# A hybrid decoder layer on one core: fixed buffers for the gated values, the merge's product in halves, and another place for a norm's iteration

## The chip, the cores and the metric

The kernel runs on one core of a Trainium2 chip. Its time is the device time of one execution in microseconds. An execution drives five engines, each with its own queue of instructions that it works through in order: TensorE (PE in the profile; its weight loads are PEld), VectorE (DVE), ScalarE (ACT), GpSimd (POOL) and SyncE (SP). SyncE and GpSimd issue the DMA transfers.

## The reference

One decoder layer for 1024 prompt tokens and 8 single decode tokens, 1032 in all, in float32, with model width 1024 and FFN width 2816:

```python
def swiglu_half(x, g, w_gate, w_up, w_down):
    u = rmsnorm(x, g)
    return x + 0.5 * ((jax.nn.silu(u @ w_gate) * (u @ w_up)) @ w_down)
...
    h = swiglu_half(x, lp['ffn1_norm'], lp['ffn1_w_gate'], lp['ffn1_w_up'], lp['ffn1_w_down'])
    u = rmsnorm(h, lp['mix_norm'])
    z = u @ lp['w_in']
...
    merged = (jax.nn.sigmoid(ga) * (o_att @ lp['w_branch_att'])
              + jax.nn.sigmoid(gr) * (o_ret @ lp['w_branch_ret']))
    h = h + merged @ lp['w_out']
    h = swiglu_half(h, lp['ffn2_norm'], lp['ffn2_w_gate'], lp['ffn2_w_up'], lp['ffn2_w_down'])
    gate = jax.nn.sigmoid(rmsnorm(h, lp['ple_norm']) @ lp['w_ple_gate'])
    h = h + gate * (p_emb @ lp['w_ple_proj'])
```

Between the first FFN and the merge stand latent attention and retention, which the change doesn't touch; a final norm ends the layer.

## The kernel before

Activations lie transposed, features on the 128 partitions and tokens along the free dimension. The tokens are in two halves of 516, `tp` 0 and 1, and each half in two pieces of `HC` = 258 columns, so that a piece fills one of the 8 PSUM banks. A float32 product is made of three matmuls (high by high, high by low, low by high); ScalarE takes the high part of a weight row (L106) and VectorE the low part (L107). `Rows` and `Stream` hold the weights that are ahead: SyncE fetches a raw row (L317, into one of 8 buffers of a pool), it is split into one of 6 `w` buffers, and `take` hands it out.

**The FFN block** (class `Block`, run twice, as block 1 and block 2). Its first two of 22 feature blocks go through a plain product, in four steps n = 0 to 3 that are (l, tp) = (0,0), (1,0), (1,1), (0,1) (L562 to L564); the others go through `unit`, a product by a Strassen-like scheme with 7 instead of 8 multiplications (L337 to L340), whose operands are sums of token blocks, made on VectorE (L509 to L517) and split (L107) into `b0` for tp 0 and `b1` for tp 1. The RMS norm's scale is applied to the results. `norm(tp)` has two steps: the first sums the squares on TensorE (L355) and finds the inverse root by an iteration of twelve tiny steps on VectorE (L357, L146 to L150); the second spreads it over the partitions by TensorE (L364) and copies it to `r` by ScalarE (L366). The norm of tp 1 takes its first step ahead of step n = 2 and its second behind n = 2's products.

The gated values are written to HBM, `mid_d`, from four `s` tiles (L541), since they don't fit beside the operands. The down product (`product`, L384 to L386) reads them back as 22 tiles `m` of 516 KB each: for tp 0 GpSimd fetches them, f = 0 first, and for tp 1 SyncE, each into the buffer that tp 0 has done with (L703). For each f the product makes 24 matmuls, three for each of 8 banks. The pool of the `m` tiles is opened when `b0`, `b1`, the x1 copy of the tokens and the `s` tiles are closed, and lies over them; a fetch waits until what lay at its buffer's place has been used for the last time.

**The merge** makes the gated mix of the two branches (L1453, L1454), keeps it for tp 0 in SBUF and writes it for tp 1 to HBM (`mg_d`). Its product with `w_out` runs for each tp over four quarters of 256 output columns, four banks each, in 8 steps f. After the first quarter of tp 0 it asks for all eight operands of tp 1 (`operand`, L1420) and for tp 1's residual (`residual`, L1424). A quarter's results are added to the residual (L1484) and stored to `h2_d` (L1486). While tp 1 is multiplied, the norm, the tokens' scaling (L499) and the sums of tp 0 for block 2 are made step by step.

The order on each engine comes from a scheduler of the framework, which works from the order of the program and its own estimates; at run time each engine keeps that order.

Of the kernel before, what the change touches and what calls it, by code (L numbers as in the profile page):

```python
# [10 lines left out]
F32 = mybir.dt.float32  # L11
F32R = mybir.dt.float32r
# [8 lines left out]
P = 128  # L21
D = 1024
KT = D // P
# [6 lines left out]
NF = DFF // P  # L30
# [19 lines left out]
HC = T // 4  # L50
TPS = (0, 1)
# [5 lines left out]
def body(ctx, tc, a):  # L57
# [370 lines left out]
    class Block:  # L428
# [100 lines left out]
        def run(self, nxt, nxt_st, prepare, accs=None, load=None, more=None):  # L529
# [38 lines left out]
                return self.pe.tile([P, HC], F32, tag="p", name="p")  # L568

            for n, (l, tp) in enumerate(((0, 0), (1, 0), (1, 1), (0, 1))):  # L570
                norm = None
                if n == 2 and accs[tp] is not None:
                    norm = self.norm(tp, accs[tp])
                    next(norm)
                if n == 0 and not begun:
                    rows.ahead, ws, pg = 0, [], []
                    for lr in range(2):
                        load(0, lr)
                        self.fresh(0, lr)
                        ws += [rows.take() for _ in range(2)]  # L580
                        pg.append(plain(ws[:2], 0, lr))
                    load(1, None)
                    squared(0)
                    rows.ahead = 3
                else:
                    if n != 2:
                        ws = [rows.take() for _ in range(4)]
                    pg = [plain(ws[:2], tp, lr) for lr in range(2)]
                if n == 0 and accs[tp] is not None:
                    norm = self.norm(tp, accs[tp])  # L590
                    next(norm)
                pu = [plain(ws[2:], tp, lr) for lr in range(2)]
                if norm:
                    next(norm)
                ts = []
                for lr in range(2):
                    t = pt()
                    ts.append(t)
                    dve.tensor_tensor(t, pg[lr][:, :HC], self.r[tp][:, HV[lr]], op=ALU.mult)
                    act.activation(t, t, AF.Silu)  # L600
                for lr in range(2):
                    dve.tensor_tensor(ts[lr], pu[lr][:, :HC], ts[lr], op=ALU.mult)
                    put(0, tp, l, lr, ts[lr])
                if n == 0:
                    if not begun:
                        squared(1)
                    for _ in self.plain_tokens(1):
                        pass
                elif n == 1:
                    if not begun:  # L610
                        self.scaled(0)
                        for _ in self.sums(0):
                            pass
                    self.last_sum(0)
                elif n == 2:
                    for _ in self.sums(1):
                        pass
# [77 lines left out]

            nxt.open()
            m_st = ExitStack()
            mp = m_st.enter_context(pools(pre + "m", NF, side="right"))
            mids = {}

            def fetch(tp, f):
                mids[tp, f] = t = mp.tile([P, 2, 2 * HC], F32R, tag="m", name="m")
                self.loaded = (sp if tp else pool).dma_start(t.bitcast(F32), self.mid_d[f, tp])  # L703

            for f in range(NF):
                fetch(0, f)
            with pools(pre + "h", 2) as hp, pools(pre + "t", 2) as tmp:
                for tp in TPS:
                    for o in range(2):
                        ht = hp.tile([P, 4, 2 * HC], F32, tag="h", name="h")  # L710

                        def each(f):
                            if f == 4:
                                sp.dma_start(ht, self.src[:, 4 * o:4 * o + 4, both(tp)])
                            if (tp, o) == (0, 1):
                                fetch(1, f)

                        end = tp == 1 and o == 1
                        if end:
                            next(nxt.norms[0])  # L720
                        banks = product(rows, lambda f: mids[tp, f], NF, 4, each)
                        if tp == 1 and o == 0:
                            with tc.issue_after(self.loaded.ins):
                                nxt.first = prepare(nxt.ring)
                        if end:
                            m_st.close()
                            nxt.open_u(nxt_st)
                            nxt.fetch()
                            next(nxt.norms[0])
                        for n in range(8):  # L730
                            hv = ht[:, n // 2, HV[n % 2]]
                            t = tmp.tile([P, HC], F32, tag="c", name="c")
                            dve.scalar_tensor_tensor(t, banks[n][:, :HC], 0.5, self.r[tp][:, HV[n % 2]],
                                                     op0=ALU.mult, op1=ALU.mult)
                            dve.tensor_tensor(hv, hv, t, op=ALU.add)
                            if n % 2:
                                k = 4 * o + n // 2
                                sp.dma_start(self.dst[:, k:k + 1, both(tp)], ht[:, n // 2:n // 2 + 1])
                        if tp == 1 and o == 0:
                            held = ht  # L740
                        if end:
                            for k in range(4):
                                nxt.row(tmp, 1, k, held[:, k])
                        for k in range(4):
                            if tp == 0 or end:
                                nxt.row(tmp, tp, 4 * o + k, ht[:, k])
                        for k in range(4):
                            nxt.squares(tmp, tp, 4 * o + k, ht[:, k], dve if end else pool)
                        if end and more:
                            more()  # L750
# [663 lines left out]
    wms = [wm_st.enter_context(pools("wm0", KT))]  # L1414
    xs = {}

    def operand():
        for f in range(KT):
            xs[1, f] = t = wms[1].tile([P, 2, 2 * HC], F32R, tag="wm", name="wm")
            sp.dma_start(t.bitcast(F32), mg_d[f])  # L1420

    def residual(tp):
        for k in range(0, KT, 4):
# [2 lines left out]
    with pools("mt", 2) as mt:  # L1426
# [14 lines left out]
        for j, (tp, o, lr) in enumerate(todo):  # L1441
            if j + 5 < len(todo):
                fetch(*todo[j + 5])
            if j == 16:
                rows = Rows(two.wp, two.rawp, [a["wout"][f][:, o_ * 256:o_ * 256 + 256]
                                               for _ in TPS for o_ in range(4) for f in range(KT)], 3)
            elif j > 24 and j % 2:
                rows.ahead_one()
            sg, mr = gates.pop((tp, o, lr))
            ps = bank()  # L1450
            proj(ps[:, :HC], wa[o // 2], oat, cols(tp, lr), off=(o % 2) * 512)
            m = mt.tile([P, HC], F32, tag="m", name="m")
            dve.tensor_tensor(m, ps[:, :HC], sg, op=ALU.mult)  # L1453
            dve.tensor_tensor(m, m, mr, op=ALU.add)  # L1454
            if lr == 0:
                if tp == 0:
                    xs[0, o] = st = wms[0].tile([P, 2, 2 * HC], F32R, tag="wm", name="wm")
                else:
                    st = mt.tile([P, 2, 2 * HC], F32R, tag="mst", name="mst", bufs=4)
            split(st[:, 0, HV[lr]], st[:, 1, HV[lr]], m)  # L1460
            if tp == 1 and lr == 1:
                sp.dma_start(mg_d[o], st.bitcast(F32))
# [7 lines left out]
    sums_of = []  # L1470
    for tp in TPS:
        sums_of.append(two.accs())
        for o in range(4):
            def each(f):
                if steps is not None and (o > 0 or f in (1, 5)):
                    next(steps, None)
            banks = product(rows, lambda f: xs[tp, f], KT, 2, each)
            if tp == 0 and o == 0:
                operand()
                residual(1)  # L1480
            for n in range(4):
                k = 2 * o + n // 2
                hv = two.hts[tp][:, k, HV[n % 2]]
                dve.tensor_tensor(hv, banks[n][:, :HC], hv, op=ALU.add)  # L1484
                if n % 2:
                    sp.dma_start(h2_d[:, k:k + 1, both(tp)], two.hts[tp][:, k:k + 1])  # L1486
            for k in (2 * o, 2 * o + 1):
                two.sq(sums_of[tp], k, two.hts[tp][:, k])
        if tp == 0:
            steps = chain(two.norm(0, sums_of[0]), two.plain_tokens(0), two.sums(0))  # L1490
# [223 lines left out]
```

## Time and profile before

| | |
|---|---|
| median of 3 runs | 2540.04 us (2535.09 to 2541.17) |
| the profiled execution | 2543.56 us |
| its span in the trace | 2540.8 us |
| granted TensorE clock, mean | 0.985 |
| TensorE busy | 2453.4 us |
| VectorE busy | 1471.0 us |
| ScalarE busy | 958.7 us |
| mean DMA rate | 136 GB/s |

Rows of the waits view name the engine, the tile and line that waited, what released it, and then the sum in us, the number of waits and the longest. Rows of the timeline give start and length in us, engine, line, operation and tiles (written <- read), the number of instructions that the row stands for, and in brackets the idle time just before and what ended it. An engine name with a q behind it is its DMA issuing. A row of the windows view gives the stretch and its length, then busy time with number of instructions for PE, PEld, DVE, ACT and POOL, then the granted TensorE clock, the share of the DMA engines and GB/s.

### The profile page before, as it was taken

The page shows a single profiled execution, that of the slowest core. Times are in us where ns is not written, and L with a number is a line of the kernel's source. Part 1 is how long each engine was busy: PE and PEld are TensorE (multiplying, and loading weights), DVE is VectorE, ACT ScalarE, POOL GpSimd, SP SyncE. Part 2 cuts the span into 40 slices and gives each one's busy share as a digit, 9 for nine tenths or more (in the row PEclk, how much of TensorE's full clock was granted, in tenths as well). Part 3 has the DMA queues.
Part 4 walks back from the last instruction along what each step waited for, and adds up shares of the span by engine and source line. Part 5 has one row for each costly group of instructions (what it writes and reads, how often), then busy time and mean ns, then how long its engine had stood idle before and what let it go on. Part 6 is the DMA issues. An engine that isn't in the chain of part 4 may idle for free.

```text
span 2540.8 us, 48866 instructions
## 1 busy us (share of the span) xinstructions
PE 2453.4 (97%) x19132; PEld 2361.3 (93%) x19132; DVE 1471.0 (58%) x3408; ACT 958.7 (38%) x2099; POOL 183.2 (7%) x245
## 2 busy tenths in 40 slices
PE   7999999799999999999999999899999997999998
PEld 7999999799999999999985669899999997999997
DVE  8767667534533656422556776676676675335345
ACT  7444444423322111211245562454444443223221
POOL 0000000111001101100141200000000001110011
PEclk9999999899999999999999999899999998999999
DMA  4223233759622122222134429432233337695231
GB/s 164 101 88 117 90 117 115 264 215 324 219 87 99 58 69 74 88 74 89 38 91 117 120 76 313 164 134 101 84 117 106 104 125 267 215 326 196 98 116 67
DMA packets 174377, 344.69 MB, mean 136 GB/s; under 512 B 19082, under 2 KB 69667, under 8 KB 174147
## 3 DMA queue, kind: packets, MB, share of 16 engines
q1 hardware_dynamic: 162690, 304.74, 35.9%
q0 software_dynamic: 11456, 36.85, 3.8%
q8 instruction: 150, 2.46, 0.4%
q14 instruction: 81, 0.66, 0.1%
HBM read 252.88 MB, written 87.58 MB: 134 GB/s over the span
## 4 chain that ended last, share of the span: by engine, by line
PE 55%; DMA 2%; DVE 1%; issue 0%; ACT 0%; SPq 0%; POOLq 0%; POOL 0%; DVEq 0%; ACTq 0%
PE ps L141 5%; PE ps L142 5%; PE ps L143 5%; PE ps L339 5%; PE ps L337 5%; PE ps L340 5%; PE ps L384 4%; PE ps L385 4%; PE ps L386 4%; PE ps L1203 2%; PE ps L1228 2%; PE ps L1239 2%; PE ps L563 1%; PE ps L562 1%; PE ps L564 1%; PE ps L1351 1%
## 5 line engine op out<-in xcount | busy, mean ns | idle before, releaser
L339 PE MATMUL ps<-b,w 128*128 128x258 f32 x2240 | 636.6, 284 | 0.0
L337 PE MATMUL ps<-b,w 128*128 128x258 f32 x2240 | 633.1, 283 | 0.0
L340 PE MATMUL ps<-b,w 128*128 128x258 f32 x2240 | 630.2, 281 | 0.0
L384 PE MATMUL ps<-m,w 128*128 128x258 f32 x1408 | 402.5, 286 | 27.8 <-DMA m<-mid_d 26.2
L340 PEld LDWEIGHTS ps<-b,w 128*128 128x128 f32 x2240 | 427.0, 191 | 0.0
L339 PEld LDWEIGHTS ps<-b,w 128*128 128x128 f32 x2240 | 424.8, 190 | 0.0
L337 PEld LDWEIGHTS ps<-b,w 128*128 128x128 f32 x2240 | 421.5, 188 | 0.0
L385 PE MATMUL ps<-m,w 128*128 128x258 f32 x1408 | 399.2, 284 | 0.0
L386 PE MATMUL ps<-m,w 128*128 128x258 f32 x1408 | 398.6, 283 | 0.0
L107 DVE TENSOR_TENSOR w<-wd,w 128x512 fp32r<-128x512 f32 (+1 forms) x264 | 164.7, 636 | 291.6 <-ACT w L106 287.2
L141 PE MATMUL ps<-u,w 128*128 128x344 f32 (+4 forms) x960 | 312.0, 325 | 3.0 <-DMA u<-u_d 3.0
L142 PE MATMUL ps<-u,w 128*128 128x344 f32 (+4 forms) x960 | 308.1, 321 | 0.0
L143 PE MATMUL ps<-u,w 128*128 128x344 f32 (+4 forms) x960 | 307.6, 320 | 0.0
L384 PEld LDWEIGHTS ps<-m,w 128*128 128x128 f32 x1408 | 267.6, 190 | 29.6 <-issue 13.4
L106 ACT CAST w<-wd 128x512 fp32r<-128x512 f32 (+1 forms) x264 | 148.2, 566 | 366.4 <-PE ps L386 317.9
L107 DVE TENSOR_TENSOR w<-wq,w 128x512 fp32r<-128x512 f32 x264 | 181.6, 688 | 151.3 <-ACT w L106 148.9
L385 PEld LDWEIGHTS ps<-m,w 128*128 128x128 f32 x1408 | 269.0, 191 | 0.0
L386 PEld LDWEIGHTS ps<-m,w 128*128 128x128 f32 x1408 | 268.0, 190 | 0.0
L141 PEld LDWEIGHTS ps<-u,w 128*128 128x128 f32 (+1 forms) x960 | 179.9, 187 | 5.6 <-DVE u L419 3.0
L142 PEld LDWEIGHTS ps<-u,w 128*128 128x128 f32 (+1 forms) x960 | 179.6, 187 | 0.9 <-issue 0.4
L143 PEld LDWEIGHTS ps<-u,w 128*128 128x128 f32 (+1 forms) x960 | 179.7, 187 | 0.6
L106 ACT CAST w<-wq 128x512 fp32r<-128x512 f32 x264 | 163.6, 620 | 34.9 <-PE ps L340 24.4
(320 smaller groups left out, 4155.2 us busy)
## 6 DMA issues: line engine op xcount, KB each, us to landing
mid_d<-s SPq DMA_DIRECT2D x88, 516.0 KB
m<-mid_d POOLq DMA_DIRECT2D x44, 516.0 KB, 13.1
m<-mid_d SPq DMA_DIRECT2D x44, 516.0 KB
wd<-in_f1down_dram SPq DMA_DIRECT2D x88, 256.0 KB
wd<-in_f2down_dram SPq DMA_DIRECT2D x88, 256.0 KB
ct<-in_cache_dram SPq DMA_DIRECT2D x128, 128.0 KB
wq<-in_f1gate_dram SPq DMA_DIRECT2D x44, 256.0 KB
wq<-in_f1up_dram SPq DMA_DIRECT2D x44, 256.0 KB
```

The costliest lines, as they stand in the source:

```text
L106: act.copy(dst_hi, src)
L107: dve.tensor_tensor(dst_lo, src, dst_hi.bitcast(F32), op=ALU.subtract)
L141: pe.matmul(ps, w[:, 0, ws], x[:, 0, xs], start=start, stop=False)
L142: pe.matmul(ps, w[:, 0, ws], x[:, 1, xs], start=False, stop=False)
L143: pe.matmul(ps, w[:, 1, ws], x[:, 0, xs], start=False, stop=stop)
L337: pe.matmul(ps, w[:, 0, js], t[:, 0], start=q in (0, 1, 3) and j == 0, stop=False, skip_group_check=True)
L339: pe.matmul(ps, w[:, 0, js], t[:, 1], start=False, stop=False, skip_group_check=True)
L340: pe.matmul(ps, w[:, 1, js], t[:, 0], start=False, stop=j == kh - 1, skip_group_check=True)
L384: pe.matmul(ps, w[:, 0, ws], t[:, 0, HV[n % 2]], start=f == 0, stop=False)
L385: pe.matmul(ps, w[:, 0, ws], t[:, 1, HV[n % 2]], start=False, stop=False)
L386: pe.matmul(ps, w[:, 1, ws], t[:, 0, HV[n % 2]], start=False, stop=f == nf - 1)
L1203: pe.matmul(ps[:, :w], qc[hd][:, i * P:(i + 1) * P], kc[hd][:, j:j + w], start=True, stop=not diag)
```

## The change

The change has three parts.

1. **Gated values.** The pool of the `m` tiles has 22 names with one buffer each instead of one name with 22 buffers that rotate. The buffers are laid out from f = 21 to f = 0, and fetched in the old order, f = 0 first (the fetch's line is now L705). In bytes of a partition, for block 1, a tile across a border counted to what is freed later:

| place in SBUF | what lay there | before | now |
|---|---|---|---|
| 73344 to 89856 | the `s` tiles | f = 0 (at 76960), f = 19 to 21 | f = 18 to 21 (21 at 76960) |
| 89856 to 147648 | `b1`, operand of tp 1 | f = 5 to 18 | f = 4 to 17 |
| 147648 to 171552 | the x1 tokens and their norm's tiles | f = 1 to 4 (1 at 163648) | f = 0 to 3 (0 at 163648) |

GpSimd's queue has the same rows in the same order; what its fetches wait for is different: the first now waits for DMAs and splits of the plain stage alone.

2. **The merge's product.** Two halves of 512 columns with all 8 banks, instead of four quarters with 4; the weight rows are 32 of 256 KB instead of 64 of 128 KB. Operands are asked for one by one, six beside tp 0's first half and two beside its second, and the residual behind them. The steps of tp 0's norm, tokens and sums are taken one for each f but the first in tp 1's first half, and up to two for each f in its second.

3. **The norm of tp 1.** Its first step is made behind step n = 1's second product, ahead of n = 1's evacuation, and its second step between n = 2's two products.

```diff
             for n, (l, tp) in enumerate(((0, 0), (1, 0), (1, 1), (0, 1))):
-                norm = None
-                if n == 2 and accs[tp] is not None:
-                    norm = self.norm(tp, accs[tp])
-                    next(norm)
...
                     pg = [plain(ws[:2], tp, lr) for lr in range(2)]
-                if n == 0 and accs[tp] is not None:
-                    norm = self.norm(tp, accs[tp])
+                if n == 2:
+                    next(norm)
+                norm = None
+                if n == 0 and accs[0] is not None:
+                    norm = self.norm(0, accs[0])
                     next(norm)
                 pu = [plain(ws[2:], tp, lr) for lr in range(2)]
                 if norm:
+                    next(norm)
+                if n == 1:
+                    norm = self.norm(1, accs[1])
                     next(norm)
...
-            mp = m_st.enter_context(pools(pre + "m", NF, side="right"))
+            mp = m_st.enter_context(pools(pre + "m", side="right"))
+            def mid(tp, f):
+                mids[tp, f] = mp.tile([P, 2, 2 * HC], F32R, tag=f"m{f}", name="m")
+
+            def fetch(tp, f):
+                self.loaded = (sp if tp else pool).dma_start(mids[tp, f].bitcast(F32), self.mid_d[f, tp])
+
+
             mids = {}
-
-            def fetch(tp, f):
-                mids[tp, f] = t = mp.tile([P, 2, 2 * HC], F32R, tag="m", name="m")
-                self.loaded = (sp if tp else pool).dma_start(t.bitcast(F32), self.mid_d[f, tp])
-
+            for f in reversed(range(NF)):
+                mid(0, f)
             for f in range(NF):
                 fetch(0, f)
...
                             if (tp, o) == (0, 1):
+                                mid(1, f)
                                 fetch(1, f)
...
-    def operand():
-        for f in range(KT):
-            xs[1, f] = t = wms[1].tile([P, 2, 2 * HC], F32R, tag="wm", name="wm")
-            sp.dma_start(t.bitcast(F32), mg_d[f])
+    def operand(f):
+        xs[1, f] = t = wms[1].tile([P, 2, 2 * HC], F32R, tag="wm", name="wm")
+        sp.dma_start(t.bitcast(F32), mg_d[f])
...
-                rows = Rows(two.wp, two.rawp, [a["wout"][f][:, o_ * 256:o_ * 256 + 256]
-                                               for _ in TPS for o_ in range(4) for f in range(KT)], 3)
+                rows = Rows(two.wp, two.rawp, [a["wout"][f][:, o_ * 512:o_ * 512 + 512]
+                                               for _ in TPS for o_ in range(2) for f in range(KT)], 3)
...
-        for o in range(4):
+        for o in range(2):
             def each(f):
-                if steps is not None and (o > 0 or f in (1, 5)):
-                    next(steps, None)
-            banks = product(rows, lambda f: xs[tp, f], KT, 2, each)
-            if tp == 0 and o == 0:
-                operand()
-                residual(1)
-            for n in range(4):
-                k = 2 * o + n // 2
+                if tp == 0 and o == 0 and f > 1:
+                    operand(f - 2)
+                elif tp == 0 and o == 1 and f < 2:
+                    operand(f + 6)
+                elif tp == 0 and o == 1 and f == 2:
+                    residual(1)
+                if steps is not None:
+                    for _ in range((f > 0) + (o > 0)):
+                        next(steps, None)
+            banks = product(rows, lambda f: xs[tp, f], KT, 4, each)
+            for n in range(8):
+                k = 4 * o + n // 2
...
-            for k in (2 * o, 2 * o + 1):
+            for k in range(4 * o, 4 * o + 4):
                 two.sq(sums_of[tp], k, two.hts[tp][:, k])
```

How the change moves instructions, at two places. SyncE's queue in the merge, before (`wd` are raw weight rows, `wm` operands of tp 1, `ht<-hs_d` its residual, `h_d<-ht` stores of results):

```order
L317 DMA wd<-in_wout_dram 128x256 x6
L1420 DMA wm<-mg_d_166 128x1032
L1420 DMA wm<-mg_d_167 128x1032
L1420 DMA wm<-mg_d_168 128x1032
L1420 DMA wm<-mg_d_169 128x1032
L1420 DMA wm<-mg_d_170 128x1032
L1420 DMA wm<-mg_d_171 128x1032
L1420 DMA wm<-mg_d_172 128x1032
L1420 DMA wm<-mg_d_173 128x1032
L1424 DMA ht<-hs_d 128x4x516 x2
L1486 DMA h_d<-ht 128x516 x2
L317 DMA wd<-in_wout_dram 128x256 x15
```

Now, from the fifth of the eight operands on:

```order
L1426 DMA wm<-mg_d_170 128x1032
L317 DMA wd<-in_wout_dram 128x512
L1426 DMA wm<-mg_d_171 128x1032
L1496 DMA h_d<-ht 128x516 x4
L317 DMA wd<-in_wout_dram 128x512
L1426 DMA wm<-mg_d_172 128x1032
L317 DMA wd<-in_wout_dram 128x512
L1426 DMA wm<-mg_d_173 128x1032
L317 DMA wd<-in_wout_dram 128x512
L1430 DMA ht<-hs_d 128x4x516 x2
L317 DMA wd<-in_wout_dram 128x512 x9
L1496 DMA h_d<-ht 128x516 x4
```

A weight row now stands between any two operands, the residual behind the last of them, and four stores together at each half's end.

VectorE's queue in the plain stage of block 1, before, around the first step of tp 1's norm (L357 takes TensorE's sums from a bank; `b_199` is tp 0's operand, `b_204` tp 1's):

```order
L107 TENSOR_TENSOR b_199<-ht,b_199 128x4x258
L517 TENSOR_TENSOR ht<-ht 128x4x258
L107 TENSOR_TENSOR b_199<-ht,b_199 128x4x258
L357 TENSOR_SCALAR sv<-ps_696 128x6
L107 TENSOR_TENSOR b_199<-ht,b_199 128x4x258
L146 TENSOR_SCALAR sz<-sv 128x6
L509 TENSOR_TENSOR ht<-ht 128x4x258
L148 TENSOR_TENSOR st<-sv,sz 128x6
L107 TENSOR_TENSOR w<-wd,w 128x512
L149 SCALAR_TENSOR_TENSOR st<-st,sz 128x6
L511 TENSOR_TENSOR ht<-ht 128x4x258
L150 SCALAR_TENSOR_TENSOR sz<-st,sz 128x6
```

Now:

```order
L107 TENSOR_TENSOR b_204<-ht,b_204 128x4x258
L107 TENSOR_TENSOR s<-p,s 128x258
L107 TENSOR_TENSOR b_204<-ht,b_204 128x4x258
L357 TENSOR_SCALAR sv<-ps_662 128x6
L601 TENSOR_TENSOR p<-ps_587,r_190 128x258
L146 TENSOR_SCALAR sz<-sv 128x6
L490 TENSOR_SCALAR ht<-ht,gains 128x516
L148 TENSOR_TENSOR st<-sv,sz 128x6
L490 TENSOR_SCALAR ht<-ht,gains 128x516
L107 TENSOR_TENSOR w<-wd,w 128x512
L149 SCALAR_TENSOR_TENSOR st<-st,sz 128x6
L490 TENSOR_SCALAR ht<-ht,gains 128x516
```

L357 stood behind the sums of tp 0 (the last of them, L517, is seen above) and now stands ahead of them; the iteration runs among the scalings L490 and ends ahead of them too. On TensorE the norm's second step (L364) stood 168 matmuls behind the sums of squares (L355) in block 1 and now stands 96 behind; in block 2 it is 48 instead of 96. The sum for the first weights of the units (L267), which stood among tp 1's token sums, now stands behind the last of them and behind n = 2's and n = 3's evacuations.

## The prediction, made before the changed kernel was run

> **What bounds the kernel.** I read the busy table first, then what TensorE waited for, longest first.
>
> ```profile
> PE 2453.4 (97%) x19132; PEld 2361.3 (93%) x19132; DVE 1471.0 (58%) x3408; ACT 958.7 (38%) x2099; POOL 183.2 (7%) x245
> PE ps L384 <- DMA m<-mid_d: 26.2, 2, 13.3
> PE ps L384 <- ACT w L106: 12.1, 1, 12.1
> PE ps L562 <- ACT b L484: 9.3, 1, 9.3
> PE ps L364 <- DVE sz L150: 7.7, 2, 6.6
> ```
>
> TensorE is busy for 97% of the span. The change adds and removes no matmul, so what there is to gain is idle time, and four waits hold most of it: two on the gated values `m` (one per FFN block), one on a weight split in the merge, one in the norm. The 9.3 us are the start of the program and stay. The other three are what the three parts of the change touch.
>
> A long wait also costs something after it. Two windows of TensorE, with the granted clock in the column before the DMA share:
>
> ```profile
> 492.20:496.70 4.50, 4.50 (x21) 4.50 (x22) 0.00 (x0) 0.00 (x0) 1.23 (x3) 0.50 1.03 414
> 498.00:520.00 22.00, 22.00 (x185) 22.00 (x184) 5.54 (x8) 4.40 (x8) 5.83 (x11) 1.00 1.03 407
> 1567.00:1586.00 19.00, 18.74 (x152) 18.38 (x152) 5.86 (x16) 4.39 (x13) 0.00 (x0) 1.00 0.97 357
> 1586.00:1598.00 12.00, 0.08 (x1) 0.08 (x1) 1.08 (x3) 0.54 (x2) 0.00 (x0) 0.63 0.89 320
> 1598.00:1603.00 5.00, 5.00 (x24) 5.00 (x25) 3.52 (x10) 2.56 (x7) 0.00 (x0) 0.53 0.64 199
> ```
>
> Behind the gap that ends at 492.2 the clock is 0.50 and 21 matmuls take 4.50 us (0.214 each); from 498 on it is 1.00 and 185 take 22.00 (0.119 each). The slow start costs 21 x 0.095 = 2.0 us. In the merge it is 24 x (0.208 - 0.119) = 2.1 us.
>
> **Part 1: the gated values.** The rows are SyncE's, GpSimd's and TensorE's around the end of block 1's units; the last is block 2's.
>
> ```profile
> 460.83 1.26 SPq L541 DMA_DIRECT2D mid_d<-s  x2
> 462.15 18.01 SPq L317 DMA_DIRECT2D wd<-in_f1down_dram  x13
> 480.50 1.26 SPq L541 DMA_DIRECT2D mid_d<-s  x2
> 485.36 4.36 POOL L703 DMA_DIRECT2D m<-mid_d  x8 [484.88 <-DMA mid_d<-s]
> 479.01 0.28 PE L340 MATMUL ps<-b,w 128*128 128x258 f32 x1
> 492.20 0.58 PE L384 MATMUL ps<-m,w 128*128 128x258 f32 x1 [12.91 <-DMA m<-mid_d]
> 2141.08 0.55 PE L384 MATMUL ps<-m,w 128*128 128x258 f32 x1 [13.27 <-DMA m<-mid_d]
> ```
>
> GpSimd's first fetch (f = 0) issues at 485.36, when the last write from the `s` tiles has landed, because f = 0's buffer lies over them. The 21 others stand behind it in GpSimd's queue, though their own data is older. Landing takes until 492.2; TensorE was through at 479.3. After the change the same queue order finds f = 0 to 3 on the x1 copy, free since the plain stage; f = 4 to 17 on the tp 1 operand `b`, free when the last tp 1 unit ends (its write-out issues at 460.83); and only f = 18 to 21 on the `s` tiles, free near 485. The product takes 24 matmuls for each f, 24 x 0.119 = 2.9 us, so f = 4 is wanted at 479.3 + 11.6 = 491 and f = 18 at 531. From 460.8 on, 14 fetches of 516 KB and 13 weight rows of 256 KB are 7.4 + 3.4 = 10.8 MB, at the 407 GB/s that the window from 498 shows 26.5 us: all landed by 487, ahead of f = 4. Both gaps go, with their slow starts: 12.9 + 2.0 and 13.3 + 2.0 = 30.2. What is late next: the first bank's release by the last unit's evacuation, taken as 0.1 each. **-30.0 us.** From both sides: nothing better than -30.2; should the weight rows, which share the queues with the early fetches, come late, a wait of some us returns (below).
>
> [...] The fetches here issue in about 0.53 us each beside VectorE's tensor_tensor work, and no run here shows more; a doubled issue time would stay inside the slack and leave the sum as it is.
>
> **Part 2: the merge's product.** SyncE, ScalarE and VectorE:
>
> ```profile
> 1569.22 3.94 SPq L317 DMA_DIRECT2D wd<-in_wout_dram  x6
> 1573.20 6.90 SPq L1420 DMA_DIRECT2D wm<-mg_d  x8
> 1580.87 1.60 SPq L1424 DMA_DIRECT2D ht<-hs_d  x2
> 1583.42 3.67 SPq L1486 DMA_DIRECT2D h_d<-ht  x2
> 1587.18 14.97 SPq L317 DMA_DIRECT2D wd<-in_wout_dram  x15
> 1597.46 2.27 ACT L106 CAST w<-wd 128x256 fp32r<-128x256 f32 x6 [17.99 <-DMA wd<-in_wout_dram]
> 1596.45 0.49 DVE L499 TENSOR_SCALAR ht<-ht,gains 128x516 f32<-128x516 f32 x1 [15.99 <-DMA h_d<-ht]
> ```
>
> The weight rows for the second quarter stand in SyncE's queue behind eight operands (4.2 MB), the residual (2.1 MB) and two stores; they issue at 1587.18 and land ten us later, with the DMA share at 0.89 to 0.97. After the change a weight row goes out between any two operands, 23 us of product (8 f x 2.9) stand before the second half instead of 11.5 before the second quarter, and the residual for tp 1 comes when tp 0 is nearly done. By the end of a half its successors' rows have had 15 us or more. So the 12.15 us wait goes, and its slow start: -12.15 - 2.1 = -14.2. New is that a half fills all 8 banks, so the next half's first matmul waits for an evacuation.
>
> ```profile
> 1613.63 1.50 DVE L1484 TENSOR_TENSOR ht<-ps,ht 128x258 f32<-128x258 f32 x4 [0.29 <-PE ps L386]
> 1614.45 1.04 SPq L1486 DMA_DIRECT2D h_d<-ht  x2
> 625.19 0.39 PE L384 MATMUL ps<-m,w 128*128 128x258 f32 x1 [0.55 <-DVE c L733]
> ```
>
> An evacuation takes 0.37 us per bank and TensorE's three matmuls per bank 0.36, so only the first is waited for. The nearest row is the FFN product's boundary with 8 banks and two VectorE operations per bank: 0.55. Two boundaries inside the tps, one between them and the norm's sums, which need a bank too, make +1.0 in all. From both sides: 0 if VectorE is free at each; +5 if SyncE, held by four stores behind the last evacuation (8 x 0.37 = 3.0, and twice 1.04 to issue), makes the next weight row late. I take 1.0, by the row of the like boundary, since rows are split several f ahead. **-13.2 us.** The larger first rows (2 MB rather than 1) load earlier, among the gates, where their splits lie under matmuls.
>
> **Part 3: tp 1's norm.** First the norm's VectorE steps and TensorE's rows in block 1, then windows in which VectorE's busy time is the figure behind the second bracket, then the same steps in block 2.
>
> ```profile
> 38.06 0.47 PE L355 MATMUL ps<-ones,acc 128*128 128x1 f32 x3
> 55.20 0.16 DVE L357 TENSOR_SCALAR sv<-ps 128x6 f32<-128x6 f32 x1
> 65.75 0.15 DVE L150 SCALAR_TENSOR_TENSOR sz<-st,sz 128x6 f32<-128x6 f32 x1
> 65.96 0.80 PE L364 MATMUL ps<-ident,sz 128*128 128x128 f32 x2 [6.60 <-DVE sz L150]
> 72.94 0.68 DVE L107 TENSOR_TENSOR w<-wq,w 128x512 fp32r<-128x512 f32 x1
> 75.22 0.28 PE L339 MATMUL ps<-b,w 128*128 128x258 f32 x1
> 42.00:66.00 24.00, 17.40 (x146) 17.20 (x144) 24.00 (x38) 12.38 (x18) 0.00 (x0) 0.94 0.20 67
> 66.00:76.00 10.00, 10.00 (x68) 10.00 (x69) 9.26 (x18) 6.33 (x15) 0.00 (x0) 0.80 0.24 79
> 1700.00:1710.00 10.00, 10.00 (x86) 10.00 (x85) 2.78 (x11) 1.77 (x3) 0.00 (x0) 1.00 0.29 106
> 1699.24 0.17 DVE L357 TENSOR_SCALAR sv<-ps 128x6 f32<-128x6 f32 x1
> 1701.47 0.17 DVE L150 SCALAR_TENSOR_TENSOR sz<-st,sz 128x6 f32<-128x6 f32 x1
> ```
>
> The sums are done at 38.5, but VectorE comes to L357 only at 55.20, and its iteration ends at 65.9. After the change L357 stands behind the operand split near 39.5, and the iteration, among some 10 us of other work, ends near 50.5. TensorE comes to L364 96 matmuls after the sums, at 38.5 + 96 x 0.12 = 50.0: that wait shrinks to some tenths. But VectorE is full from 42 to 66 and nearly so to 76, with the same work before and after. Its weight splits for the first unit are done near 72.5 (the second of them at 72.94 now) either way, and TensorE, earlier by 6.6 + 1.9, would reach the units at 66.7. The stall moves there: start at 72.5 instead of 75.22 is 2.7 won, less a new slow start after a wait of 5.8 us, 1.2 to 2.0. **-1.5 us.** From both sides: -8.5 if the splits go ahead of the sums; +1 if they come at 74.5, since L267 stands behind more evacuations than it did. I take the near end because VectorE shows no idle time to pay from. In block 2 the same norm has no wait now; its two steps get 48 matmuls between them (5.8 us), where VectorE took 2.4 (1699.24 to 1701.64) with little beside it: 0, and +2 if other work of VectorE comes between.
>
> **Sum.** -30.0 - 13.2 - 1.5 = -44.7. The profiled execution took 2543.56 (span 2540.8), so it would take 2498.9. It lies 3.5 above the median of the runs, 2540.04; against that: **2495.4 us**.
>
> **Rivals.**
> A. The norm's stall goes whole, 7 us more: 2488.4. For it: VectorE is busy for only 2.78 of 10 us behind the same norm in block 2. Against: the full windows of block 1. 0.12.
> B. Something is paid back: the merge's stores hold SyncE (+4), or the first down rows come late among the early fetches and half of one mid wait returns (+6), or the norm costs +3: 2499 to 2508, middle 2504. For it: a DMA share of 1.03 at 498 to 520, which now begins 25 us earlier. Against: the 26.5 us above. 0.17.
> C. The change doesn't do what it says: one of the fetches ahead in GpSimd's queue still waits for the last `s` write, and both mid waits stay: 2495.4 + 30.0 = 2525.4. Against: no early slot lies on those tiles. 0.05.
> D. Slower: with the rests gone, the granted clock falls. The mean is 0.985 over 2453.4 us of matmuls; at a mean c they take 2453.4 x 0.985/c. The 44.7 us are gone at c = 0.967, and below 0.964 the kernel is slower by over 0.3%: at 0.960 64 us come back, 2559.
>
> ```profile
> PEclk9999999899999999999999999899999998999999
> ```
>
> Against it: of the 40 slices only those from 445, 1588 and 2096 us show 8, which hold the three long waits, and the clock is 1.00 in the busy windows above: it falls in and behind gaps, not under work. [...] 0.06.
>
> **Chances and range.** The forecast itself holds 0.60: 2495.4, from 2488 to 2500. The range takes in A below (2488.4 less the scatter of the three runs, some 4) and B above to 2510: 2484 to 2510, leaving out C, D and tails, some 0.15. A measurement tells 0.3% (7.6 us) from no change. Forecast, A, B and C are faster, 0.94; D is split between within 0.3%, 0.03, and slower, 0.03.
>
> **What would show it.** Right: no wait on `m` in either block, with GpSimd's fetches issuing near 460 or earlier; no wait on a weight split in the merge; L364 in block 1 without a wait, but one of 4 to 6 us before the first unit near 66; TensorE's idle time down from 87 to some 45 us; busy time of TensorE lower by 5 or 6, by the slow starts. Wrong: a first matmul of either down product that waits for a weight split or `m`; waits over 2 us at the merge's halves; a granted clock under 0.98.

## The result, and the profile after

| | before | changed |
|---|---|---|
| median | 2540.61 us (4 runs, 2535.09 to 2542.45) | 2503.92 us (4 runs, 2503.24 to 2505.02) |
| profiled execution | 2543.56 | 2503.24 |
| span | 2540.8 | 2499.9 |
| granted clock, mean | 0.985 | 0.993 |

The ratio is 0.986, with a 95% interval of 0.9843 to 0.9877. On a second chip it was 0.9845 (0.9829 to 0.9862), from 2542.05 to 2502.09 us. The forecast was 2495.4 in a range of 2484 to 2510: the time lies in it, 8.5 us above the forecast.

The changed kernel's page, the engines' busy time and TensorE's clock by slices:

```profile
PE 2448.1 (98%) x19132; PEld 2354.9 (94%) x19132; DVE 1469.4 (59%) x3376; ACT 956.2 (38%) x2067; POOL 183.0 (7%) x245
PEclk9999999999999999999999999999999999999999
```

The top of TensorE's waits, with two smaller ones:

```profile
PE ps L562 <- ACT b L484: 9.0, 1, 9.0
PE ps L337 <- ACT w L106: 5.2, 1, 5.2
...
PE ps L337 <- DVE e L676: 2.4, 2, 1.6
...
PE ps L384 <- ACT r L366: 0.7, 1, 0.7
```

The three waits named in the prediction are gone from the list, and so are the three slices with a lower clock. TensorE's busy time fell by 5.3 us, which fits the slow starts behind those waits (2.0, 2.0 and 2.1 us in the prediction, with new ones behind new waits). Its idle time, span less busy time, fell from 87 to 52 us; 45 was forecast. New are 5.2 us before the units and 2.4 us within them. Only the first was in the forecast; the second stood among the rivals.

To see where the time went I cut the span at the first and last matmul of each stage in TensorE's timeline. The two down products hold the wait ahead of them:

| stage, us | before | changed | difference |
|---|---|---|---|
| start | 9.32 | 9.00 | -0.3 |
| block 1, plain stage and units | 469.97 | 469.69 | -0.3 |
| block 1, down product | 272.07 | 257.41 | -14.7 |
| projection, attention, retention | 813.39 | 815.11 | +1.7 |
| merge's product | 110.00 | 96.38 | -13.6 |
| block 2, plain stage and units | 453.06 | 454.12 | +1.1 |
| block 2, down product | 272.25 | 257.79 | -14.5 |
| rest | 140.74 | 140.41 | -0.3 |

The sum is -40.9. The fourth row is not touched by the change; over the twelve profiled executions of this study it takes between 808.5 and 815.1 us, in no order that follows the edits, so 1 or 2 us in a total say little. For one code the two rows with units repeat within 0.8 us, the start within 1.0, the merge's within 1.2, the rest within 1.5, and a down product with its wait within 1.6. Verdicts below rest on the stage that an edit touches.

GpSimd's fetches in the changed kernel (timeline, block 1):

```profile
69.46 1.23 POOL L705 DMA_DIRECT2D m<-mid_d  x2 [68.98 <-DVE s L107]
113.66 0.53 POOL L705 DMA_DIRECT2D m<-mid_d  x1 [42.98 <-DMA mid_d<-s]
116.72 0.53 POOL L705 DMA_DIRECT2D m<-mid_d  x1 [2.53 <-DMA mid_d<-s]
456.18 4.18 POOL L705 DMA_DIRECT2D m<-mid_d  x8 [338.93 <-PE ps L340]
...
495.33 1.57 POOL L705 DMA_DIRECT2D m<-mid_d  x3 [19.32 <-DVE w L107]
```

f = 0 to 3 are fetched as soon as they have been written, near 69 to 117 us; f = 4 waits until TensorE has done with `b1`; seven more follow one by one where the dots stand, and the last three, over the `s` tiles, at 495.33. That is the order that was forecast.

### The profile page after: what moved, and what is told of

The parts are those of the page before. It is cut to its first block, busy times and chain, and to the rows that moved or that the text cites. A ratio compares the mean times of both kernels' runs of the same rounds, so it can differ in the third digit from the quotient of the medians.

```text
span 2499.9 us, 48712 instructions
## 1 busy us (share of the span) xinstructions
PE 2448.1 (98%) x19132; PEld 2354.9 (94%) x19132; DVE 1469.4 (59%) x3376; ACT 956.2 (38%) x2067; POOL 183.0 (7%) x245
## 3 DMA queue, kind: packets, MB, share of 16 engines
q1 hardware_dynamic: 158082, 304.73, 36.0%
q0 software_dynamic: 11456, 36.85, 4.2%
## 4 chain that ended last, share of the span: by engine, by line
PE 90%; DVE 4%; DMA 2%; issue 1%; SPq 1%; ACT 1%; POOLq 0%; POOL 0%; DVEq 0%; ACTq 0%
PE ps L339 10%; PE ps L337 10%; PE ps L340 10%; PE ps L384 8%; PE ps L385 8%; PE ps L386 8%; PE ps L141 8%; PE ps L142 7%; PE ps L143 7%; PE ps L1210 2%; PE ps L1235 1%; PE ps L1246 1%; PE ps L562 1%; PE ps L563 1%; PE ps L564 1%
## 5 line engine op out<-in xcount | busy, mean ns | idle before, releaser
L107 DVE TENSOR_TENSOR w<-wd,w 128x512 fp32r<-128x512 f32 x232 | 161.0, 703 | 277.4 <-ACT w L106 269.0
L106 ACT CAST w<-wd 128x512 fp32r<-128x512 f32 x232 | 142.8, 620 | 338.8 <-PE ps L386 277.7
L107 DVE TENSOR_TENSOR w<-wq,w 128x512 fp32r<-128x512 f32 x264 | 181.4, 689 | 147.3 <-ACT w L106 144.9
```

Source lines behind the costliest of these rows:

```text
L106: act.copy(dst_hi, src)
L107: dve.tensor_tensor(dst_lo, src, dst_hi.bitcast(F32), op=ALU.subtract)
```

## The experiments

**The three parts alone.** Each of the first three kernels is the kernel before with one part of the diff shown above, the rest left as it was.

> The kernel before with part 1 alone (22 names for the gated values, laid out in reverse). Theory: this part gives 26 of the 40 us, 12.6 in block 1 and 13.4 in block 2: a time near 2514 us, no wait on m, and the same small waits in the last units that the changed kernel shows (1.65 and 0.39 us near 475, 0.79 us near 2100), because the early fetches themselves cause them, by taking DMA time from the first down rows. Rival: those small waits come from the other parts; then they are missing here and the part gives 29 us, 2511.

> The kernel before with part 2 alone (output product in halves, operands singly). Theory: its gain doesn't depend on the other parts: -13.6 us, near 2527, waits at the halves under 1 us. Rival: part of it was due to block 2's other waits; then it is under 10 or over 17.

> The kernel before with part 3 alone (tp 1's norm earlier). Theory: the 6.6 us wait at L364 turns into a wait of 5.2 us at the units' second weights; what is left is 2.3 us less at the start of the units, within 0.3% of the kernel before. Rival: the whole stall of 6.6 us and its slow start go, 8.5 us, near 2532.

| | median, us | ratio (95% interval) | stage that it touches, against before |
|---|---|---|---|
| before, same chip | 2540.48 (13 runs) | | |
| slots alone | 2514.77 (4 runs) | 0.9906 (0.9889 to 0.9922) | down products -14.6 and -14.5; units +2.4 and +0.8 |
| merge alone | 2527.81 (4 runs) | 0.9954 (0.9938 to 0.9971) | merge's product -13.5 |
| norm alone | 2538.51 (10 runs) | 0.9992 (0.9982 to 1.0002) | block 1's plain stage and units -1.7 |

The three medians fall by 25.7, 12.7 and 2.0 us, 40.4 together; the whole change gave 36.7 on one chip and 40.0 on another. The parts add up within their uncertainty, and the rivals that had them depend on each other fall. The norm's part is too small for its medians, whose interval takes in no change; only its stage shows it. The slots' part brings its own small waits in the last units (2.2 us in two waits for an evacuation), as the theory had it.

**The place or the names.** The `m` buffers keep their 22 names, laid out from f = 0:

```diff
-            for f in reversed(range(NF)):
+            for f in range(NF):
                 mid(0, f)
```

> The changed kernel with the 22 named buffers laid out from f = 0 to f = 21 instead of in reverse. Theory: the place decides, not the names; f = 0 lies over the s tiles again, both waits on m come back at about 13 us, with their slow starts, and the small waits in the last units go: 2504 + 26 = 2530. Rival: a buffer with a name of its own is enough, and the time stays at 2504.

One run took 2523.82 us. Its timeline on GpSimd, and then its longest entry of TensorE's waits:

```profile
483.08 0.69 POOL L705 DMA_DIRECT2D m<-mid_d  x1 [482.60 <-DMA mid_d<-s]
```

```profile
PE ps L384 <- DMA m<-mid_d: 27.5, 2, 14.3
```

The first fetch waits for the last write from the `s` tiles again, and both waits are back: 271.85 and 272.90 us for the down products, while the units lose their small waits (453.06 in block 2, as before). The place decides, not the names. The time lies 6 us under the expected 2530; the untouched middle, 808.5 us in this run and 815.1 in the changed kernel's profile, accounts for it.

**What costs 2 us in the last units.** In the changed kernel, windows of the time in which the units end and, below, ScalarE, VectorE and TensorE there:

```profile
456.00:460.00 4.00, 4.00 (x35) 4.00 (x35) 4.00 (x9) 2.88 (x7) 3.82 (x8) 1.00 0.62 179
460.00:470.00 10.00, 10.00 (x85) 10.00 (x85) 8.34 (x17) 5.98 (x13) 2.47 (x5) 1.00 1.01 373
470.00:478.00 8.00, 5.96 (x47) 5.55 (x47) 3.98 (x9) 3.23 (x7) 1.59 (x3) 1.00 1.03 407
```

```profile
471.24 0.62 ACT L106 CAST w<-wd 128x512 fp32r<-128x512 f32 x1 [1.95 <-DMA wd<-in_f1down_dram]
475.24 0.62 ACT L106 CAST w<-wd 128x512 fp32r<-128x512 f32 x1 [1.37 <-DMA wd<-in_f1down_dram]
475.89 0.69 DVE L107 TENSOR_TENSOR w<-wd,w 128x512 fp32r<-128x512 f32 x1 [0.50 <-ACT w L106]
476.50 0.42 DVE L676 TENSOR_TENSOR e<-e,ps 128x258 f32<-128x258 f32 x1
476.97 0.39 PE L337 MATMUL ps<-b,w 128*128 128x258 f32 x1 [1.65 <-DVE e L676]
```

Read from below: TensorE waits for a bank; the evacuation that frees it (L676) stands on VectorE behind the split of a down weight (L107); that waits for ScalarE's half of it, and this for the row's DMA. The DMA share is 1.01 to 1.03. Before, in the same place, it was 0.63 and 0.69:

```profile
460.00:470.00 10.00, 10.00 (x86) 10.00 (x85) 9.96 (x21) 6.52 (x15) 0.00 (x0) 1.00 0.63 213
470.00:479.00 9.00, 9.00 (x77) 9.00 (x76) 6.72 (x15) 5.78 (x13) 0.00 (x0) 1.00 0.69 203
```

So the fetches that now come early would be what delays a weight row, which nobody in that moment needs for a matmul, but behind which an evacuation stands. To test it, only f = 0 to 7 are fetched early by GpSimd; the others are asked for on SyncE's queue during the product:

```diff
-                self.loaded = (sp if tp else pool).dma_start(mids[tp, f].bitcast(F32), self.mid_d[f, tp])
+                self.loaded = (sp if tp or f > 7 else pool).dma_start(mids[tp, f].bitcast(F32), self.mid_d[f, tp])
...
-            for f in range(NF):
+            for f in range(8):
                 fetch(0, f)
...
+                            if (tp, o) == (0, 0) and f + 8 < NF:
+                                fetch(0, f + 8)
                             if (tp, o) == (0, 1):
```

**What costs 5.2 us before the units.** The prediction said that VectorE was full and the norm's stall would only move. The changed kernel's timeline there, of TensorE, VectorE and ScalarE:

```profile
49.21 1.44 PE L364 MATMUL ps<-ident,sz 128*128 128x128 f32 x12
63.01 1.23 DVE L517 TENSOR_TENSOR ht<-ht 128x1032 f32<-128x1032 f32 x1
69.45 0.68 DVE L267 TENSOR_TENSOR ws<-wq 128x512 f32<-128x512 f32 x1
70.17 0.62 ACT L106 CAST w<-ws 128x512 fp32r<-128x512 f32 x1 [0.19 <-DVE ws L267]
65.38 0.28 PE L339 MATMUL ps<-b,w 128*128 128x258 f32 x1
70.84 0.58 PE L337 MATMUL ps<-b,w 128*128 128x258 f32 x1 [5.18 <-ACT w L106]
```

L364 has no wait, and the units begin at 65; their second weight is the sum L267, which VectorE makes only at 69.45. Whether it is late because VectorE is full or because it stands behind the evacuations of n = 3 can't be seen here. So its place is changed:

```diff
                     if n != 2:
                         ws = [rows.take() for _ in range(4)]
+                    if n == 3:
+                        stream = self.stream()
+                        for _ in range(2):
+                            stream.ahead_one()
...
-            stream = self.stream()
```

The two edits ran alone and together, beside the changed kernel, on one chip:

> The changed kernel itself, on the same chip as the next three, as their base. Both theories: near 2504 us; the waits of 5.2 us before the units' second weights, and of 1.7 and 0.8 us in the last units, as in its first profile.

> The changed kernel with only f = 0 to 7 fetched ahead of tp 0's down product by GpSimd; f = 8 to 21 are asked for on SyncE's queue, one for each step f of the product's first half, behind weight rows. Theory: the small waits in the last units come from the early fetches, which delay the first down rows on the DMA engines; with 8 instead of 18 fetches ahead they go: unit stages of 411.7 and 404.2 us instead of 413.7 and 405.3, near 2501. Rival: VectorE's own order makes them (an evacuation behind a weight split), they stay, and f = 8 may come late in addition: 2504 to 2510.

> The changed kernel with the units' first two weights (their fetch, the sum L267 and two splits) asked for ahead of step n = 3's products instead of behind all of the plain stage. Theory: the wait of 5.2 us before the units' second weight is made by the place of L267 on VectorE, behind n = 3's evacuation; with L267 some 5 us earlier the wait falls to 1 us or less, and the units end 4 us earlier or more: near 2500. Rival (as predicted blind): VectorE is full there, the same work only changes places, another wait of about 5 us stands at the next weight or at tp 1's operand: within 1 us of 2504.

> Both edits of the last two runs together. Theory: the gains add up, near 2497. Rival: one of them is only moved into the other, 2500 or more.

| | median, us (4 runs) | ratio to before (95% interval) | block 1, plain stage and units | block 2, same | down products |
|---|---|---|---|---|---|
| changed | 2502.09 | 0.9845 (0.9829 to 0.9862) | 469.56 | 454.14 | 257.43, 257.76 |
| eight early | 2495.13 | 0.9812 (0.9796 to 0.9829) | 467.71 | 453.06 | 256.74, 256.74 |
| first weights early | 2498.29 | 0.983 (0.9813 to 0.9846) | 465.86 | 455.54 | 257.46, 257.98 |
| both | 2493.17 | 0.9802 (0.9786 to 0.9819) | 465.20 | 453.06 | 256.75, 256.74 |

With eight early the small waits are gone in both blocks, and block 2's stage is back at 453.06, the time of before. Windows of that kernel, and then the timeline of its ScalarE, in the same place, up to near the end of the units:

```profile
458.00:468.00 10.00, 10.00 (x86) 10.00 (x85) 9.96 (x21) 6.36 (x15) 0.74 (x2) 1.00 0.97 340
468.00:476.00 8.00, 8.00 (x69) 8.00 (x68) 5.72 (x13) 5.22 (x11) 0.00 (x0) 1.00 0.91 323
```

```profile
470.35 0.62 ACT L106 CAST w<-wd 128x512 fp32r<-128x512 f32 x1 [0.58 <-DMA wd<-in_f1down_dram]
471.14 0.62 ACT L106 CAST w<-wd 128x512 fp32r<-128x512 f32 x1
```

SyncE's issue of the first 13 down rows, first in the changed kernel and then with eight early:

```profile
458.97 21.91 SPq L317 DMA_DIRECT2D wd<-in_f1down_dram  x13
459.44 18.02 SPq L317 DMA_DIRECT2D wd<-in_f1down_dram  x13
```

With eight early the rows take 18.02 us again, as before the change (18.01, in the prediction's row at 462.15), instead of 21.91. Only the first split waits for its row, 0.58 us, and TensorE is busy without a break. The DMA share is still 0.91 to 0.97 there, though no row holds up a matmul. The late fetches were in time: the down products are shorter too, by 0.7 and 1.0. The stages add to 4.6 us (1.85 + 1.08 + 0.69 + 1.02); the medians differ by 7.0, and I count the 4.6 as shown. The DMA view shows who held the 16 DMA engines from 456 to 480 us: in the changed kernel the queue of GpSimd's fetches (q0) for 66.1% of their time and SyncE's (q1) for 29.1%, before SyncE's for 56.5% and GpSimd's not at all. So the two share the engines, but not the queues, which the prediction took as shared: with both edits, where 28 of GpSimd's fetches are SyncE's, q0 moves 22.05 MB in all instead of 36.85 and q1 319.53 instead of 304.73. ScalarE's waits for a weight row, 1.95 and 1.37 us while GpSimd fetches and 0.58 when it fetches less, agree.

With the first weights early the wait shrinks, in that kernel's timeline, from 5.18 us to two of 1:

```profile
65.48 0.69 DVE L267 TENSOR_TENSOR ws<-wq 128x512 f32<-128x512 f32 x1
66.26 0.62 ACT L106 CAST w<-ws 128x512 fp32r<-128x512 f32 x1 [0.28 <-DVE ws L267]
66.93 0.39 PE L337 MATMUL ps<-b,w 128*128 128x258 f32 x1 [1.07 <-ACT w L106]
68.57 0.39 PE L340 MATMUL ps<-b,w 128*128 128x258 f32 x1 [1.02 <-DVE w L107]
```

VectorE has the same work in its queue, and is as full as before (busy for all 24.00 us from 42 to 66, 23.89 in the changed kernel); n = 3's evacuations stand behind L267 now instead of ahead of it, and TensorE waits for none of them. The stage falls by 3.7 us. It was the order, not the load. In block 2 the same edit costs 1.4 us (455.54), in waits of the last units (1.59 us where the changed kernel has 0.79), and there is no norm's stall there to win back; with eight early these are gone too. Both together are the best kernel of the study, 2493.17 us, 49 under before and 9 under the changed one on that chip. In block 2 nothing is left to gain (453.06). In block 1 the two gains of 1.85 and 3.70 would give 464.0; 465.20 was measured. In the profile of both together the clock is at half speed behind the two short waits, and with the first weights early alone it is not (0.50 and 1.00 over 3.30 us, in the rows of the last section); the missing 1.2 us fit that.

**What made the merge's wait go.** The change put two things together there; each was tried without the other.

```diff
-                if tp == 0 and o == 0 and f > 1:
-                    operand(f - 2)
-                elif tp == 0 and o == 1 and f < 2:
-                    operand(f + 6)
-                elif tp == 0 and o == 1 and f == 2:
-                    residual(1)
...
             banks = product(rows, lambda f: xs[tp, f], KT, 4, each)
+            if tp == 0 and o == 0:
+                for f in range(KT):
+                    operand(f)
+                residual(1)
```

> The changed kernel with the eight operands and the residual asked for in a row again, behind tp 0's first half; the halves stay. Read from the merge's product stage (110.2 us before, 96.5 to 96.6 changed). Theory: the order in SyncE's queue made the wait, so part of it is back: six weight rows are ahead, which now last 6 x 2.9 = 17 us instead of 6 x 1.44 = 8.6, while the 6.3 MB need some 18 us from their issue; a wait of 2 to 6 us, a stage of 99 to 103 us. Rival: the halves alone did it, 97 us; or the order alone, 108 us or more.

The second kernel is the one before with the six lines that are taken away here put into `each`, and the call of `operand()` and `residual(1)` behind the first quarter taken out.

> The kernel before with the operands asked for one for each step f (six in the first quarter, two in the second, the residual behind), quarters kept. Theory: a weight row between any two operands is enough, the wait of 12 us falls to 3 us or less and the stage to 97 to 101 us, though quarters give 11.5 us of product beside 3.1 MB of operands. Rival: the halves were needed; a wait of 6 us or more stays, the stage is 104 us or longer.

The stage takes 96.25 us with halves at once (one run, 2498.51 us), 105.56 with quarters singly (one run, 2538.13), against 110.00 before and 96.38 changed; the kernel before took 2535.63 in its one run on that chip. So quarters singly won nothing in the whole time, though its stage is shorter. SyncE's queue with halves at once, and TensorE's wait with quarters singly:

```profile
1550.98 3.90 SPq L317 DMA_DIRECT2D wd<-in_wout_dram  x6
1554.93 7.33 SPq L1426 DMA_DIRECT2D wm<-mg_d  x8
1563.26 1.61 SPq L1430 DMA_DIRECT2D ht<-hs_d  x2
1568.57 2.48 SPq L1494 DMA_DIRECT2D h_d<-ht  x4
1571.14 16.64 SPq L317 DMA_DIRECT2D wd<-in_wout_dram  x13
```

```profile
PE ps L384 <- ACT w L106: 6.4, 4, 3.2
```

With halves, eight operands and the residual stand ahead of the weight rows just as before the change, and no wait comes of it. The six rows issued ahead of them are the second half's first; with the first half's eight they last for 14 f of product. By the prediction's 2.9 us for one f that is 40.6 us, so the row issued at 1571.14 is wanted only near 1587, 40.6 us after the stage's start at 1546.70. Before the change 14 smaller rows of 1.44 us lasted 20.2 us, from 1564.75 to 1585, and the next row was issued at 1587.18, after it was wanted. With quarters, a weight row between any two operands takes 4.4 us off the stage and leaves 6.4 us in four waits. My theory was wrong on both: the halves are enough by themselves, and the order of the operands added nothing to be seen beside them. That they work through the time that the rows ahead last is worked out from these rows; larger rows without the eight banks were not tried. Both results are single runs, but the stages differ by 9 us, where the merge's stage takes 95.95 to 97.13 in the eight profiled executions with halves.

## Why the prediction was right, and where it was off

| term | forecast | measured | how |
|---|---|---|---|
| gated values, both blocks | -30.0 | -26.1 | the two down products, -14.7 and -14.5, with the waits that came back in the units, +2.0 and +1.1 |
| merge | -13.2 | -13.6 | the stage |
| norm | -1.5 | -2.3 | 467.71 with eight early, free of the units' waits, against 469.97; the norm alone -1.7 |
| rest | 0 | +1.1 | start, middle and end, not touched |
| profiled execution | 2498.9 | 2503.24 | the terms give 2502.7; 0.6 lie outside the span |
| median | 2495.4 | 2503.92 | |

- **What bounds the kernel** was read rightly: idle time of TensorE behind three kinds of wait, and a slow start behind each. Busy time fell by 5.3 us; 5 or 6 were forecast.
- **Gated values.** Mechanism and place were right, the size was off by 3.9. The step that failed is "all landed by 487, ahead of f = 4": that was enough for the fetches, and TensorE waits for no `m`, but the sum of bytes was set against the first need of a fetch, not against the first need of the weight rows that share the DMA engines. Those are wanted from 470 on, and 1 to 2 us of lateness in each was passed on through VectorE's queue to a bank. It stood among the rivals, with its cause, as one way of B at 6 us; it cost 3.1, in the units and not at the mid wait. The 0.1 us for the first bank in each block had no row behind it; in the changed kernel the product's first matmuls waited for evacuations 0.26 us in block 1, 0.24 and 0.26 in block 2. Also, the down products gave 1.6 and 1.4 us beside their gaps, where the slow start was put at 2.0.
- **Merge.** The size was right within 0.5 us and the reason half wrong: of the two given, the row between any two operands and the longer product in front of the second half, the second alone was enough. The new waits of TensorE there are 0.7 us for the norm's `r` and less at the halves, 1.0 in the sum.
- **Norm.** L364 lost its wait and a stall of 5.18 us came before the units, 5.8 forecast. The slow start behind it took 3.20 us at a clock of 0.50, or 1.6 us, where the sum used 1.2, for which no row stood. But "VectorE shows no idle time to pay from" was the wrong reason: other work could stand behind the weights' sum at the same load, and one edit of the order took 3.7 us off the stage. So the forecast's -1.5 came out for this order alone, and rival A's gain was partly open. VectorE was as full with that edit as without it (24.00 and 23.89 of 24.00 us); the order decided what was late.
- **From the profile to the median.** 3.5 us were taken off because the profiled execution of before lay that much above its median. The changed kernel's lay 0.7 below its own. So the offset was one execution's scatter; this is 4.2 of the 8.5 us.
- **Rivals C and D** didn't come: no fetch that is needed early waits for the `s` tiles, and the mean clock rose from 0.985 to 0.993. GpSimd's eight fetches took 4.18 us to issue, in all of which VectorE was busy with tensor_tensor work. The eight before took 4.36, but VectorE did nothing then (0.00 us busy from 485.36 to 489.72), so the prediction's "beside VectorE's tensor_tensor work" didn't hold for that row.

## What to carry to other kernels

Where a buffer lies can cost time with the number of buffers unchanged (here 27.5 us in two waits): put the first that is needed over what is freed first. When transfers are let go earlier, look for the first need of everything that shares the DMA engines with them, and for what stands in a queue behind whoever waits for it (here 2.4 us of waits for an evacuation behind a late weight row); fetch ahead what covers the gap, no more. Where an engine is full ahead of a stall, try the order of its work before giving the stall up (here 3.7 us).

## What the runs showed of the hardware

In these runs the length of a gap of TensorE didn't tell by itself whether a slow start followed. Windows behind a gap, two pairs of the same place: first behind the wait for `u` after block 1's down product, in the changed kernel (a wait of 2.89 us) and with halves at once (2.69), then behind the two short waits in front of the units, with the first weights early (1.07 and 1.02) and with both edits (1.08 and 1.01):

```profile
741.40:745.00 3.60, 3.60 (x17) 3.60 (x18) 3.60 (x7) 0.40 (x2) 0.00 (x0) 0.50 1.06 405
742.30:745.90 3.60, 3.60 (x31) 3.60 (x32) 3.60 (x7) 0.42 (x1) 0.00 (x0) 1.00 1.03 395
69.00:72.30 3.30, 3.30 (x30) 3.30 (x29) 3.30 (x8) 2.49 (x6) 0.17 (x1) 1.00 0.25 79
69.90:73.20 3.30, 3.30 (x17) 3.30 (x17) 3.30 (x8) 2.46 (x6) 0.14 (x1) 0.50 0.29 79
```

In each pair one kernel runs 17 matmuls at a clock of 0.50 where the other runs 30 or 31 at 1.00, behind nearly the same waits; what decides between the two was not shown. In the clock records of the kernel before and of the changed kernel every stretch at one clock, but the first and the last of a run, lasts a whole number of steps of 3.41 us; those at 0.50 last 3.41, 6.83 or 13.65 us. Behind each wait of 5 to 14 us inside these two runs TensorE worked at 0.50 at first: before, for 4.14 us behind 6.60, 4.56 behind 12.91, 4.76 behind 12.15 and 4.32 behind 13.27; in the changed kernel for 3.20 behind 5.18. Cutting this last wait into two short ones saved the slow start with the first weights early alone, and not with both edits. Part of the scatter of the untouched middle can come from here too: behind the wait for `u` the changed kernel worked at 0.50 for 5.13 us, which is 2.6 us lost by my estimate, half of the 5.13, while the row with halves at once shows 1.00 there.
